# The second norm's gain: from the token rows to the experts' transposed tiles, and a second buffer for the normed rows

## The chip, the cores and the metric

The kernel runs on one core of a Trainium2 chip. The metric is the device time of one execution in microseconds (us); the median of three runs of the kernel before is 1646.28 us. The engines are named as in the profile: PE (TensorE), PEld (its weight loads), DVE (VectorE), ACT (ScalarE), POOL (GpSimd) and SP (the sync engine, which here issues most DMAs).

## What is computed

Two transformer blocks stand one after the other on 512 tokens of width 1024. The change touches the end of the second block, cut here to what matters:

```
x = x + u @ w_out                                  # output projection and residual
h = x * rsqrt(mean(x*x) + eps) * g                 # second norm, g = norm2_g (1024 weights)
logits = h @ w_router + b                          # 4 groups, 32 experts
y = sum over the token's two experts of weight * ((silu(h @ w_gate[e]) * (h @ w_up[e])) @ w_down[e])
x = x + y
```

Each token goes to two of 32 experts. An expert has 6 MB of f32 weights (gate, up and down), so that all of them are about 200 MB that stream once from HBM.

## The kernel before

**Output projection and norm (lines 1208 to 1377).** The projection runs in two column halves `c` (line 1375: `c = 0`, line 1376: `c = 1`) over four token tiles `t` of 128 tokens. For each tile `ev_o(c)` (lines 1281 to 1318) is called when the last matmul has been issued: DVE adds the PSUM result to the residual in `x2` (line 1285, called the evacuation below), ACT squares it and sums (1286), PE transposes it (`transpose4`, line 258, four matmuls), ACT copies the transpose out (1307), and PE multiplies it with the router's weights (1296, eight matmuls to a tile); for `c = 1` DVE adds the two halves' logits (1300) and scales them by the row's `rs` (1301). `rs` comes from DVE (line 251) and a power on POOL (line 252).

**Normed rows.** At `c = 1` the tile also gets a buffer `h`, with one copy in the pool (`bufs=1`). POOL multiplies its first 512 columns by the gain (line 1290) and DVE the other 512 (line 1291); `normed_rows` (lines 1273 to 1279) then scales it by `rs` in place on ACT, in two steps, writes it to the DRAM tensor `h_d` by a DMA on POOL's queue (1278), and writes the un-normed `x2` rows to the output by a DMA on ACT's queue (1279). The buffer of tile `t + 1` can be written only when the DMA of tile `t` has read it.

**Routing.** `route(a, b)` (lines 1328 to 1353) picks the experts of tiles `a` to `b - 1` on DVE, and `places` (1355 to 1372) gives every token its slot in its expert's list. Tiles 0 to 2 are routed when the logits of tile 2 are there (line 1303), tile 3 afterwards. The slot lists `gi` (line 1500) say which rows of `h_d` an expert reads.

**Experts (lines 1406 to 1655).** Weights come through SP's queue in units of 2 MB, two DMAs each (`fetch`, line 1402), into a ring of ten unit buffers (`RING = 10`). Six of the first ten lie where the projection's tiles lie or `x2` lies, so that their loads wait for those; from the eleventh unit on a load waits until PE has used the unit that lay in its buffer. For each expert POOL gathers its rows of `h_d` (line 1525, three in advance), PE transposes them (`expert_x`, 1544), DVE copies the transpose to `xT` (1547), PE multiplies with gate and up (1555) and with down (1580), and POOL adds the weighted result to the output by a scattering DMA (1532). Experts with more than 64 tokens do the same again for a second list (`gv`, `yv`). The first gathers wait for all four `h_d` writes and for `gi`. `overflow` (line 1663), for over 128 tokens in one expert, is built but not entered with these inputs.

The order on each engine is set by the program's scheduler from the dependences; PE's in the expert stage follows the code.

The lines around which all of this turns:

```
xg[t] = rt1.tile([P, D], F32, tag="h", bufs=1, name=f"h2_{t}")
nc.gpsimd.tensor_tensor(xg[t][:, 0:512], x2[:, t, 0:512], g_n2[:, 0:512], op=ALU.mult)
nc.vector.tensor_tensor(xg[t][:, 512:D], xc, g_n2[:, 512:D], op=ALU.mult)
```

Of the kernel before, what the change touches and what calls it, by code (L numbers as in the profile page):

```python
# [9 lines left out]
F32 = mybir.dt.float32  # L10
# [4 lines left out]
AF = mybir.ActivationFunctionType  # L15
ALU = mybir.AluOpType
# [4 lines left out]
P = 128  # L21
S = 512
NT = S // P
D = 1024
KD = D // P
# [62 lines left out]
def tile_kernel(tc, I, out, dbg=None, stop=None):  # L88
    nc = tc.nc
# [211 lines left out]
    def load_row(pool, ap, n, tag="grow", bufs=None):  # L301
        r = pool.tile([P, n], F32, tag=tag, bufs=bufs, name=f"row{uid()}")
        nc.sync.dma_start(r, row_bcast(ap, 0, n))
        return r
# [30 lines left out]
    for t in range(NT):  # L335
        for half in range(2):
            ps = transpose4(xt[t][:, half * 512:(half + 1) * 512])
            for j in range(4):
                k = half * 4 + j
                split(Ah[:, k, t * P:(t + 1) * P], Al[:, k, t * P:(t + 1) * P], ps[:, j * P:(j + 1) * P],  # L340
                      scale=gx[:, k:k + 1])
    for t in range(NT):
        h = hpool.tile([P, D], F32, tag="h", bufs=2, name=f"h{uid()}")
# [439 lines left out]
    for i, nm in enumerate(("attn_q_gain_2", "attn_k_gain_2")):  # L783
        for k in range(2):
# [25 lines left out]
                                     ap=[[512, 8], [-1, P], [1, 384]]))  # L810
# [120 lines left out]
    for dl in range(1, 4):  # L931
        n = NT - dl
        nc.vector.tensor_tensor(B[dl][:, :, 0:n, :], B[dl - 1][:, :, 0:n, :], tot[:, :, dl - 1:dl - 1 + n, :],
                                op=ALU.add)
# [236 lines left out]
    x2 = xp.tile([P, NT * D], F32, tag="unit", name="x2").rearrange("p (t d) -> p t d", t=NT)  # L1171
# [37 lines left out]
    SLOTS = 64  # L1209
# [22 lines left out]
    rb = rt1.tile([P, 36], F32, name="rb")  # L1232
    nc.sync.dma_start(rb[:, 0:4], row_bcast(I["b_router_group_2"], 0, 4))
    nc.sync.dma_start(rb[:, 4:36], row_bcast(I["b_router_expert_2"], 0, 32))
    g_n2 = load_row(rt1, I["norm2_g_2"], D, bufs=1)
    LG = rtp.tile([P, NT, 36], F32, name="LG")
    h_d = dram.tile([S, D], F32, name="h_d")

# [32 lines left out]
    s2 = rt1.tile([P, NT, 2], F32, name="s2")  # L1271

    def normed_rows(t):
        h = xg[t]
        for c_ in range(2):
            cl = slice(c_ * 512, (c_ + 1) * 512)
            nc.scalar.activation(h[:, cl], h[:, cl], AF.Copy, scale=rs[t])
        hw[0] = nc.gpsimd.dma_start(h_d[t * P:(t + 1) * P, :], h)
        nc.scalar.dma_start(out[0, t * P:(t + 1) * P, :], x2[:, t, :])

    def ev_o(c):

        def ev(t, ps):
            xc = x2[:, t, c * 512:(c + 1) * 512]
            nc.vector.tensor_tensor(xc, xc, ps, op=ALU.add)
            nc.scalar.activation(ps, xc, AF.Square, accum_out=s2[:, t, c:c + 1])
            hT = rt1.tile([P, 4, P], F32, tag="hT", bufs=2, name=f"hT2_{t}{c}")
            if c == 1:
                xg[t] = rt1.tile([P, D], F32, tag="h", bufs=1, name=f"h2_{t}")
                nc.gpsimd.tensor_tensor(xg[t][:, 0:512], x2[:, t, 0:512], g_n2[:, 0:512], op=ALU.mult)  # L1290
                nc.vector.tensor_tensor(xg[t][:, 512:D], xc, g_n2[:, 512:D], op=ALU.mult)

            def logits():
                lp_ = bank("s")
                for k in range(4):
                    nc.tensor.matmul(lp_[:, 0:36], hT[:, k, :], wr[:, c * 4 + k, :], start=k == 0, stop=k == 3)
                if c == 0:
                    nc.vector.tensor_copy(LG[:, t, :], lp_[:, 0:36])
                    return
                nc.vector.tensor_tensor(LG[:, t, :], LG[:, t, :], lp_[:, 0:36], op=ALU.add)  # L1300
                nc.vector.scalar_tensor_tensor(LG[:, t, :], LG[:, t, :], rs[t], rb, op0=ALU.mult, op1=ALU.add)
                if t == NT - 2:
                    route(0, NT - 1)

            def post():
                tp = transpose4(xc)
                copied = nc.scalar.activation(hT.rearrange("p j t -> p (j t)"), tp, AF.Copy)
                later(logits, 1)
                if c == 1:
                    with tc.issue_after(copied.ins):  # L1310
                        normed_rows(t)
            later(post, 1)
            if c == 0:
                return
            ss = small.tile([P, 1], F32, tag="ss", name=f"ss{uid()}")
            nc.vector.tensor_tensor(ss, s2[:, t, 0:1], s2[:, t, 1:2], op=ALU.add)
            rs[t] = rstd(ss, 1, 1.0 / D)
        return ev
# [52 lines left out]
        nc.vector.tensor_reduce(pj[:, qa:qb], prod, axis=AX.X, op=ALU.add)  # L1371
        onehots(0, io64, range(qa, qb))

    rs, hw, xg = {}, [None], {}
    run(lin_tok(A, wo_, [(0, 512)], ev_o(0), W=per_row(wo_u), beat=2))
    run(lin_tok(A, wo_, [(512, 512)], ev_o(1), W=per_row([wout(u, 1) for u in range(4)]),
                beat=2))
# [161 lines left out]
    def expert_x(xs, xT=None):  # L1539

        xv = xs.rearrange("s (p j) -> s j p", j=4)
        tp = tr_bank("xt")
        for j in range(4):
            nc.tensor.transpose(tp[:, j * P:(j + 1) * P], xv[:, j, :], ident)  # L1544
        if xT is None:
            xT = mp.tile([P, 4, P], F32, tag="xT", bufs=2, name=f"xT{uid()}")
        nc.vector.tensor_copy(xT.rearrange("p j s -> p (j s)"), tp)  # L1547
        return xT

    def gu_half(ps, xT, W, h):  # L1550
# [109 lines left out]
    tb_i = dram.tile([NE, P], I32, name="tb_i")  # L1660
    tb_w = dram.tile([NE, P], F32, name="tb_w")

    def overflow(blk):
        tb = ops.tile([P, 512], F32, tag="tr", name=f"tb{blk}")
        onehots(blk * P, iota, range(2 * NT))
# [6 lines left out]
        with tc.For_i(0, NE, 1) as i:  # L1672
# [9 lines left out]
            for half in range(2):  # L1682
                tp = ops.tile([P, 512], F32, tag="tr", name=f"otp{blk}{half}")
                for j in range(4):
                    nc.tensor.transpose(tp[:, j * P:(j + 1) * P], xv[:, half * 4 + j, :], ident)
                nc.vector.tensor_copy(xT[:, half * 4:half * 4 + 4, :].rearrange("p j s -> p (j s)"), tp)
            gu = []
            for nm, w_ in (("g", wg_d), ("u", wu_d)):
                w = op.tile([P, KD, 512], F32, tag="w" + nm, name=f"ow{nm}{blk}")
# [64 lines left out]
```

## Time and profile before

| what | value |
|---|---|
| runs | 1644.40, 1646.28, 1648.93 us; median 1646.28 |
| the profiled execution | 1646.24 us, its span 1644.5 us |
| PE busy | 1510.2 us (92%) |
| DVE, ACT, POOL busy | 695.5 us (42%), 537.3 us (33%), 200.7 us (12%) |
| DMA | 320.91 MB, mean 195 GB/s |
| DMA share in the last 12 of 40 slices | 90% or more but for the very last |

The span is what the hardware profiler recorded; the execution's own time is 1.7 us longer than it. Busy shares are averages over stages with different limits: the first two thirds are matmuls at full rate, the last third is the stream of expert weights. A releaser in brackets or behind an arrow is what ended an engine's idle time.

### The profile page before, as it was taken

What the parts mean: (1) busy time and instruction counts of PE and PEld (TensorE: products, weight loads), DVE (VectorE), ACT (ScalarE), POOL (GpSimd) and SP (SyncE); (2) the same over time, 40 slices, a digit from 0 to 9 for tenths busy, and PEclk for the clock granted to TensorE, in tenths of its full rate; (3) what the DMA queues carried; (4) which work ended last, traced back from release to release, by engine and by line L of the source; (5) the groups of instructions that cost most, each with busy time, mean ns of one, the idle gap of its engine ahead of it and who ended that gap; (6) DMA issues with size and microseconds to landing.
All of it is one profiled execution on the core that took longest, in us unless ns stands there. A gap on an engine that the chain in (4) does not pass through costs nothing. (4 is left out here: it accounts for less than half of the span.)

```text
span 1644.5 us, 20717 instructions
## 1 busy us (share of the span) xinstructions
PE 1510.2 (92%) x7446; PEld 1044.7 (64%) x7446; DVE 695.5 (42%) x1545; ACT 537.3 (33%) x1044; POOL 200.7 (12%) x196
## 2 busy tenths in 40 slices
PE   7999999889999999989999999993989999998875
PEld 7887776688888888778888778783333333333231
DVE  7699636663334454556884454624100100000000
ACT  6444437742234343344454543231111011111000
POOL 1000001220000000140000000003222222322211
PEclk9999999999999999999999999996999999999998
DMA  5313105013333332234222235397799999999995
GB/s 175 116 52 90 40 26 179 27 52 102 103 103 103 103 102 91 84 103 149 89 71 65 83 110 208 105 386 292 295 406 412 408 410 409 402 409 409 412 414 213
DMA packets 100064, 320.91 MB, mean 195 GB/s; under 512 B 18532, under 2 KB 27316, under 8 KB 75362
## 3 DMA queue, kind: packets, MB, share of 16 engines
q1 hardware_dynamic: 88626, 306.63, 50.0%
q0 software_dynamic: 10736, 10.54, 2.6%
q10 hardware_dynamic: 576, 2.10, 0.3%
q8 instruction: 75, 1.23, 0.3%
q14 instruction: 51, 0.42, 0.1%
HBM read 317.07 MB, written 21.25 MB: 206 GB/s over the span
## 5 line engine op out<-in xcount | busy, mean ns | idle before, releaser
L126 PE MATMUL mm<-wh,Ah 128*128 128x512 f32 (+3 forms) x800 | 307.8, 385 | 7.5 <-ACT wh L132 3.7
L127 PE MATMUL mm<-wl,Ah 128*128 128x512 f32 (+3 forms) x800 | 299.8, 375 | 1.2 <-DVE wl L133 1.2
L128 PE MATMUL mm<-wh,Al 128*128 128x512 f32 (+3 forms) x800 | 299.7, 376 | 0.0
L1555 PE MATMUL gu<-mr,xT 128*64 128x512 f32 x1024 | 240.4, 611 | 36.4 <-DMA mr<-in_w_expert_up_dram 21.4
L133 DVE TENSOR_TENSOR wl<-raw,wh 128x1024 fp32r<-128x1024 f32 (+3 forms) x160 | 184.8, 1162 | 118.2 <-ACT wh L132 114.8
L132 ACT ACTIVATE wh<-raw 128x1024 fp32r<-128x1024 f32 (+3 forms) x164 | 163.9, 1008 | 143.9 <-PE mm L127 108.6
L1555 PEld LDWEIGHTS gu<-mr,xT 128*64 128x64 f32 x1024 | 77.3, 140 | 174.4 <-issue 169.1
L126 PEld LDWEIGHTS mm<-wh,Ah 128*128 128x128 f32 x800 | 152.5, 191 | 34.3 <-ACT wh L132 4.8
L126 PE MATMUL mm<-Ah,wh 128*128 128x512 f32 x416 | 169.4, 407 | 0.0
L127 PEld LDWEIGHTS mm<-wl,Ah 128*128 128x128 f32 x800 | 153.0, 191 | 24.8 <-DVE wl L133 2.2
L128 PEld LDWEIGHTS mm<-wh,Al 128*128 128x128 f32 x800 | 152.3, 191 | 25.7 <-DVE Al L133 0.7
L128 PE MATMUL mm<-Ah,wl 128*128 128x512 f32 x416 | 163.2, 392 | 0.0
L127 PE MATMUL mm<-Al,wh 128*128 128x512 f32 x416 | 163.2, 392 | 0.0
L1547 DVE COPY xT<-xt 128x512 f32<-128x512 f32 x35 | 24.2, 692 | 307.1 <-PE xt L1544 307.1
L252 POOL TENSOR_TENSOR rr<-rm,mhalf 128x1 f32<-128x1 f32 (+3 forms) x40 | 32.5, 813 | 920.8 <-DVE rm L251 917.5
L1580 PE MATMUL yy<-mr,aT 128*64 128x512 f32 x512 | 116.9, 597 | 9.7 <-PEq L1643 8.4
L1580 PEld LDWEIGHTS yy<-mr,aT 128*64 128x64 f32 x512 | 39.4, 136 | 85.4 <-issue 81.2
L127 PEld LDWEIGHTS mm<-Al,wh 128*128 128x128 f32 x416 | 78.3, 188 | 17.6 <-issue 2.9
L126 PEld LDWEIGHTS mm<-Ah,wh 128*128 128x128 f32 x416 | 78.4, 188 | 17.2 <-issue 2.9
L1532 POOL DMA_INDIRECT out_dram<-ys,gi x35 | 56.3, 1608 | 268.0 <-ACTq L1606 202.7
L128 PEld LDWEIGHTS mm<-Ah,wl 128*128 128x128 f32 x416 | 78.3, 188 | 15.9
L1572 ACT ACTIVATE aT<-at 128x256 f32<-128x256 f32 x35 | 13.4, 382 | 160.5 <-PE at L1570 160.3
(370 smaller groups left out, 1860.4 us busy)
## 6 DMA issues: line engine op xcount, KB each, us to landing
mr<-in_w_expert_gate_dram SPq DMA_DIRECT2D x64, 1024.0 KB, 21.0
mr<-in_w_expert_up_dram SPq DMA_DIRECT2D x64, 1024.0 KB
mr<-in_w_expert_down_dram SPq DMA_DIRECT2D x64, 1024.0 KB, 21.2
raw<-in_w_in_dram SPq DMA_DIRECT2D x56, 512.0 KB, 3.6
raw<-in_w_up_dram SPq DMA_DIRECT2D x32, 512.0 KB, 3.7
raw<-in_w_down_dram SPq DMA_DIRECT2D x32, 512.0 KB, 4.1
raw<-in_w_out_dram SPq DMA_DIRECT2D x16, 512.0 KB, 4.3
gate_d<-gt SPq DMA_DIRECT2D x16, 256.0 KB, 2.9
```

Source lines behind the costliest of these rows:

```text
L126: nc.tensor.matmul(ps, ah, bh, start=first, stop=False)
L127: nc.tensor.matmul(ps, ah, bl, start=False, stop=False)
L128: nc.tensor.matmul(ps, al, bh, start=False, stop=last)
L132: nc.scalar.activation(hi, src, AF.Copy)
L133: return lo_eng.tensor_tensor(lo, src, hi.bitcast(F32), op=ALU.subtract)
L252: nc.gpsimd.tensor_tensor(r[:, :n], m[:, :n], mhalf[:, :n], op=ALU.pow)
L1532: nc.gpsimd.indirect_dma_start(out=dst, out_offset=bass.IndirectOffsetOnAxis(ap=idx, axis=0), in_=ys, in_offset=None, bounds_check=n - 1, ...
L1547: nc.vector.tensor_copy(xT.rearrange("p j s -> p (j s)"), tp)
L1555: last = nc.tensor.matmul(ps[c * 64:(c + 1) * 64, :].rearrange("s (w f) -> s w f", w=2), xT[:, j, h * 64:(h + 1) * 64], wv[:, :, j, c * 25 ...
L1572: nc.scalar.activation(aT.rearrange("p j s -> p (j s)"), tp[:, 0:256], AF.Copy)
L1580: nc.tensor.matmul(ps[c * 64:(c + 1) * 64, :], aT[:, j, h * 64:(h + 1) * 64], wv[:, h, j, c * 512:(c + 1) * 512], start=h + j == 0, stop=h ...
```

## The change

The gain is no longer multiplied into the normed rows. `normed_rows` makes the rows in one ACT step from `x2` into a buffer `h` with two copies, and the write of `x2` to the output is issued behind that step. The POOL and DVE multiplications and the load of the gain as a row on all partitions go. Instead the gain is applied where an expert's tokens have been transposed: the copy to `xT` becomes a multiplication by `g_x`, a tile of 4 by 2 gains to a partition that is repeated along the slots. `g_x` is loaded as single elements on SP's queue. The `overflow` code gets its own gain tile `g_o`, loaded at the end whether that code is entered or not. The router's weights had the gain multiplied in before and are not touched.

```
-    g_n2 = load_row(rt1, I["norm2_g_2"], D, bufs=1)
+    g_ap = I["norm2_g_2"]
+
+    def gain(pool, J, hs, nm):
+
+        g_ = pool.tile([P, J, hs], F32, name=nm)
+        nc.sync.dma_start(g_, bass.AP(tensor=g_ap.tensor, offset=g_ap.offset, ap=[[J, P], [1, J], [D // hs, hs]]))
+        return g_
+
+    g_x = gain(rtp, 4, 2, "g_x")
...
     def normed_rows(t):
-        h = xg[t]
-        for c_ in range(2):
-            cl = slice(c_ * 512, (c_ + 1) * 512)
-            nc.scalar.activation(h[:, cl], h[:, cl], AF.Copy, scale=rs[t])
+
+        h = rt1.tile([P, D], F32, tag="h", bufs=2, name=f"h2_{t}")
+        rows = nc.scalar.activation(h, x2[:, t, :], AF.Copy, scale=rs[t])
         hw[0] = nc.gpsimd.dma_start(h_d[t * P:(t + 1) * P, :], h)
-        nc.scalar.dma_start(out[0, t * P:(t + 1) * P, :], x2[:, t, :])
+        with tc.issue_after(rows.ins):
+            nc.scalar.dma_start(out[0, t * P:(t + 1) * P, :], x2[:, t, :])
...
-            if c == 1:
-                xg[t] = rt1.tile([P, D], F32, tag="h", bufs=1, name=f"h2_{t}")
-                nc.gpsimd.tensor_tensor(xg[t][:, 0:512], x2[:, t, 0:512], g_n2[:, 0:512], op=ALU.mult)
-                nc.vector.tensor_tensor(xg[t][:, 512:D], xc, g_n2[:, 512:D], op=ALU.mult)
...
-        nc.vector.tensor_copy(xT.rearrange("p j s -> p (j s)"), tp)
+        nc.vector.tensor_tensor(xT.rearrange("p j (h s) -> p j h s", h=2), tp.rearrange("p (j h s) -> p j h s", j=4, h=2),
+                                g_x[:, :, :, None].to_broadcast([P, 4, 2, SLOTS]), op=ALU.mult)
...
+    g_o = gain(op, KD, 1, "g_o")
...
-                nc.vector.tensor_copy(xT[:, half * 4:half * 4 + 4, :].rearrange("p j s -> p (j s)"), tp)
+                nc.vector.tensor_tensor(xT[:, half * 4:half * 4 + 4, :], tp.rearrange("p (j s) -> p j s", j=4),
+                                        g_o[:, half * 4:half * 4 + 4, :].to_broadcast([P, 4, P]), op=ALU.mult)
```

How the instructions stand, at three places. POOL, tiles 2 and 3 of the last projection half, before (`h_2` and `h_3` are the normed rows, `row` the gain, `rr` the power that gives `rs`, `xs` the first gather's buffer):

```order
L1290 TENSOR_TENSOR h_2_9496<-x_8767,row_9142 128x512
L252 TENSOR_TENSOR rr_9502<-rm_9501,mhalf 128x1
L1278 DMA h_d<-h_2_9496 128x1024
L1290 TENSOR_TENSOR h_3_9568<-x_8767,row_9142 128x512
L252 TENSOR_TENSOR rr_9574<-rm_9573,mhalf 128x1
L1278 DMA h_d<-h_3_9568 128x1024
L1590 MEMSET xs_9743 128x512
```

and POOL at the same place with the change:

```order
L252 TENSOR_TENSOR rr_9493<-rm_9492,mhalf 128x1
L1285 DMA h_d<-h_2_9509 128x1024
L252 TENSOR_TENSOR rr_9562<-rm_9561,mhalf 128x1
L1285 DMA h_d<-h_3_9571 128x1024
L1595 MEMSET xs_9731 128x512
```

The multiplication that stood ahead of each power is gone; nothing takes its place on POOL.

DVE, from the last step of routing tiles 0 to 2 over the evacuation of tile 3 (the row with `mm`) to that tile's logits, before (`ss` and `rm` lead to `rs`; `ohe`, `ohs`, `rec` and `recw` are routing work of tiles 0 to 2):

```order
L1347 TENSOR_TENSOR eid<-eid,gix 128x6
L1285 TENSOR_TENSOR x_8767<-x_8767,mm_9505 128x512
L1349 TENSOR_TENSOR ohe<-iota,eid 128x192
L1291 TENSOR_TENSOR h_3_9568<-x_8767,row_9142 128x512
L1353 TENSOR_TENSOR ohs<-ohe 128x96
L1316 TENSOR_TENSOR ss_9571<-s_9174 128x1
L1365 TENSOR_TENSOR rec<-ohe,tokc 128x192
L251 TENSOR_SCALAR rm_9573<-ss_9571 128x1
L1300 TENSOR_TENSOR LG<-LG,s_9587 128x36
L1369 TENSOR_TENSOR recw<-ohe,s_9175 128x64
L1301 SCALAR_TENSOR_TENSOR LG<-LG,rr_9574,rb 128x36
```

and DVE at the same place with the change:

```order
L1351 TENSOR_TENSOR eid<-eid,gix 128x6
L1293 TENSOR_TENSOR x_8767<-x_8767,mm_9496 128x512
L1353 TENSOR_TENSOR ohe<-iota,eid 128x192
L1357 TENSOR_TENSOR ohs<-ohe 128x96
L1369 TENSOR_TENSOR rec<-ohe,tokc 128x192
L1320 TENSOR_TENSOR ss_9559<-s_9174 128x1
L251 TENSOR_SCALAR rm_9561<-ss_9559 128x1
L1304 TENSOR_TENSOR LG<-LG,s_9575 128x36
L1373 TENSOR_TENSOR recw<-ohe,s_9175 128x64
L1305 SCALAR_TENSOR_TENSOR LG<-LG,rr_9562,rb 128x36
```

The write into `h_3` is gone from between the evacuation and the statistics; the evacuation still stands behind the routing of tiles 0 to 2.

SP, where the small constants and the first loads of the output projection's weights (`raw`) are issued, as a piece of the difference:

```order
 L148 DMA raw_9014<-in_w_branch_mlstm_dram 128x2x512
-L1243 DMA iota<-in_cst_dram 128x128
-L1245 DMA io_9148<-in_cst_dram 128x128
-L1247 DMA half_9150<-in_cst_dram 128x1
-L1249 DMA tokc<-in_cst_dram 128x4
-L1255 DMA recw<-in_cst_dram 128x128
+L1240 DMA g_x<-in_norm_g_dram 128x8x1
+L1251 DMA iota<-in_cst_dram 128x128
+L1253 DMA io_9148<-in_cst_dram 128x128
+L1255 DMA half_9150<-in_cst_dram 128x1
+L1257 DMA tokc<-in_cst_dram 128x4
+L1263 DMA recw<-in_cst_dram 128x128
```

The load of `g_x`, 8 single elements to each of 128 partitions, stands ahead of five small loads and of the `w_out` loads behind them; the row load of the gain, further down in the same queue, is gone.

## Rows read from the trace of the kernel before

**Rows 1.** Stretches: length, busy us of engines, PEclk, DMA share, GB/s.

```profile
1036.50:1039.00 2.50, 2.50 (x13) 2.00 (x12) 1.80 (x4) 0.63 (x1) 0.00 (x0) 1.00 1.06 227
1108.00:1113.00 5.00, 4.33 (x20) 3.25 (x19) 2.86 (x6) 0.74 (x2) 1.86 (x2) 1.00 0.02 10
1119.00:1149.00 30.00, 7.24 (x42) 6.35 (x42) 15.40 (x82) 4.29 (x9) 9.26 (x13) 0.58 0.95 353
1149.50:1161.00 11.50, 8.19 (x28) 3.15 (x30) 2.04 (x4) 0.42 (x1) 3.76 (x4) 0.63 0.21 50
1180.00:1460.00 280.00, 257.09 (x1179) 95.88 (x1180) 24.21 (x44) 30.64 (x65) 74.52 (x60) 1.00 1.02 408
1460.00:1600.00 140.00, 115.13 (x508) 42.77 (x506) 10.01 (x18) 13.77 (x28) 32.55 (x26) 0.97 1.02 412
```

**Rows 2.** Timeline of SP's queue, weight loads: start, us, instruction.

```profile
1118.66 0.33 SPq L1414 DMA_DIRECT2D mr<-in_w_expert_gate_dram  x1
...
1159.63 0.81 SPq L1414 DMA_DIRECT2D mr<-in_w_expert_down_dram  x2
```

**Rows 3.** SP's waits, 1060 to 1170: us in total, times, longest.

```profile
SPq L148 <- DVE wl L133: 30.6, 4, 25.6
SPq L1414 <- DMA out_dram<-x: 22.1, 3, 11.1
SPq L1414 <- PEq L1624: 16.1, 1, 16.1
```

**Rows 4.** Timeline of POOL: start, us, instruction, idle before it.

```profile
1101.56 0.79 POOL L1278 DMA_DIRECT2D h_d<-h  x1 [1.69 <-ACT h L1277]
...
1121.47 0.61 POOL L1278 DMA_DIRECT2D h_d<-h  x1 [1.66 <-ACT h L1277]
...
1134.93 0.60 POOL L1278 DMA_DIRECT2D h_d<-h  x1 [1.66 <-ACT h L1277]
...
1145.23 1.12 POOL L1525 DMA_INDIRECT xs<-h_d,gi  x1 [7.16 <-DVE wgt L1468]
```

**Rows 5.** Timeline of PE, tile 2's transposes and the first expert's matmuls.

```profile
1113.17 0.66 PE L258 MATMUL t<-ident,x 128*128 128x128 f32 x4 [0.84 <-DVE x L1285]
...
1153.75 5.75 PE L1555 MATMUL gu<-mr,xT 128*64 128x512 f32 x16 [0.78 <-DVE xT L1547]
```

**Rows 6.** Timeline of DVE, tiles 0 to 3 of the projection's second half.

```profile
1097.35 0.69 DVE L1285 TENSOR_TENSOR x<-x,mm 128x512 f32<-128x512 f32 x1 [2.64 <-PE mm L128]
...
1101.64 0.26 DVE L1301 SCALAR_TENSOR_TENSOR LG<-LG,rr,rb 128x36 f32<-128x36 f32 x1
1104.18 0.69 DVE L1285 TENSOR_TENSOR x<-x,mm 128x512 f32<-128x512 f32 x1 [2.29 <-PE mm L128]
...
1119.84 0.26 DVE L1301 SCALAR_TENSOR_TENSOR LG<-LG,rr,rb 128x36 f32<-128x36 f32 x1 [0.64 <-POOL rr L252]
...
1122.82 0.68 DVE L1285 TENSOR_TENSOR x<-x,mm 128x512 f32<-128x512 f32 x1
...
1130.23 1.76 DVE L1291 TENSOR_TENSOR h<-x,row 128x512 f32<-128x512 f32 x1 [6.47 <-DMA h_d<-h]
...
1133.30 0.26 DVE L1301 SCALAR_TENSOR_TENSOR LG<-LG,rr,rb 128x36 f32<-128x36 f32 x1 [0.51 <-POOL rr L252]
...
1140.39 0.25 DVE L1500 TENSOR_SCALAR gi<-t,half 128x32 int32<-128x32 f32 x1 [0.71 <-PE t L1476]
```

**Rows 7.** Groups of DVE by line and shape: busy us, mean ns, idle before.

```profile
L1547 DVE COPY xT<-xt 128x512 f32<-128x512 f32 x35 | 24.2, 692 | 307.1 <-PE xt L1544 307.1
...
L395 DVE TENSOR_TENSOR t<-mm,cs 128x512 f32<-128x512 f32 x16 | 11.0, 687 | 22.4 <-PE mm L128 22.4
...
L1291 DVE TENSOR_TENSOR h<-x,row 128x512 f32<-128x512 f32 x4 | 6.0, 1512 | 15.0 <-DMA h_d<-h 15.0
```

**Rows 8.** The DMAs that write or read h_d, time to landing.

```profile
DMA to landing us min/median/max: 2.2/7.0/9.4
```

**Rows 9.** SP's waits, 1600 to the end.

```profile
SPq L1750 <- DMA out_dram<-ys,gi: 9.2, 1, 9.2
```

More of the change, by code (lines that the diff above doesn't have):

```diff
@@ L1372, in places @@
         onehots(0, io64, range(qa, qb))
-    rs, hw, xg = {}, [None], {}
+    rs, hw = {}, [None]
     run(lin_tok(A, wo_, [(0, 512)], ev_o(0), W=per_row(wo_u), beat=2))
```

## The prediction, made before the changed kernel ran

> **What bounds the kernel now.** I read the page's slices first, where DMA share is full for the last third, then cut that third into stretches [rows 1]. From 1180 to 1460 us, and again to 1600, the DMA share stays at 1.02 and 408 to 412 GB/s: the stage moves expert weights as fast as DMA goes anywhere in this trace, while PE has some slack (257.1 of 280 us busy, then 115.1 of 140). The end of the kernel is therefore the moment from which this stream runs without holes, plus a fixed amount of bytes. So the place to look is where the stream has holes ahead of 1180. There are two. One is 1108 to 1113 (share 0.02): the next unit buffer is still read by the output projection, and its load starts only at 1118.66 [rows 2]. The other is 1149.5 to 1161 (share 0.21): all ten unit buffers are full, SP waits 16.1 us for PE [rows 3], and the next load goes out at 1159.63 [rows 2], when PE has done the first 16 matmuls of the first expert. Those began at 1153.75 and took 5.75 us [rows 5]: PE had little to do before (7.2 of 30 us), and its granted clock there is 0.58 and 0.63, mostly the lower of its two levels, 1.2 GHz [rows 1].
>
> So what is late is PE's first expert. It needs the first gather, which POOL issues at 1145.23 [rows 4]. The gather needs the slot list, there at 1140.64, and the last write of normed rows, issued at 1134.93: it waits for the write. Both are late for one reason. Of tiles 0 to 3 on DVE [rows 6], the second evacuation follows the first by 6.83 us, PE's pace; but tile 3's comes at 1122.82, not at 1117.84, and its logits end in a step at 1133.30, 10.48 us behind, where tile 0 needed 4.29. In between DVE sits 6.47 us until the DMA of the previous tile's rows has read the only buffer; over the tiles this costs DVE 15.0 us of waiting [rows 7].
>
> **The change, part by part.**
>
> *Multiplications into the buffer.* Four on POOL and four on DVE go, and with them the wait for the buffer. DVE had run late since tile 1, and PE stood 0.84 us for it [rows 5]; that goes too. New times, from tile 0's undisturbed steps [rows 4, 6]. Evacuation of tile 2: 1104.18 + 6.83 = 1111.01. Its logits' last step: + 4.29 = 1115.30. Routing of tiles 0 to 2 stays ahead of tile 3 on DVE and takes 1122.82 - 1119.84 = 2.98, so tile 3's evacuation comes at 1118.28, behind its PSUM at 1117.84. Its logits: 1122.57, which is 10.7 us earlier. The slot list: 1140.64 - 1133.30 = 7.34 later, 1129.91. The write of its rows: tile 0 took 1101.56 - 1097.35 = 4.21, so 1122.49, which is 12.4 us earlier.
>
> *One ACT step in place of two, from x2.* It does the same 1024 columns, inside the 4.21 just used; I count nothing, and at most it saves a part of that. Its result goes into one of two buffers: tile 3 wants the one that tile 1's write (issued about 1108.4) reads, 12 us after that; the slowest write seen took 10.3 (below).
>
> *Landing of the last write.* Not shown for the new conditions. Issued at 1121.47, tile 2's let DVE go at 1130.23, 8.8 us; tile 3's let the gather go 10.3 us after 1134.93 [rows 4, 6]. I take 8.8: like the new one it starts when the weight loads have just resumed. The gather goes at 1131.25, 14.0 us earlier; with 10.3 at 1132.79, 12.4 earlier; if the write were quick the slot list would decide, 1129.91, 15.3 earlier.
> The Trainium skill, SBUF — State Buffer, section "SBUF: two separate sides", says that a DMA from GpSimd's queue has its descriptors written by GpSimd, and that VectorE work on the shared ports keeps it from writing them. VectorE runs the same dense routing work beside the new write as beside the old one, so by this rule the landing stays at 10.3 and the time comes out at about 1635.0. The 8.8 of tile 2, which had VectorE idle for most of it, does not contradict that.
>
> *The gather's own flight.* From issue to the first expert's matmuls 1153.75 - 1145.23 = 8.5 us. Now it falls wholly among weight loads, where before these ended soon after. DMAs on h_d land in 7.0 us (median), at most 9.4 [rows 8]; I add 1.2, bounds 0 and 2.8. PE's first expert starts 12.8 us earlier, near 1141, still at the lower clock since PE again has some 20 us with little to do, and the first buffer is free at 1146.8.
>
> *What the stream can take of it.* Starting PE earlier pays only while the ring is full. The hole is worth 11.5 x (1 - 0.21) = 9.1 us. The fill ends earlier, too: PE's last matmul by 0.84, and tile 2's two writes of 0.5 MB (rows and output) now go out about 1115, in the empty stretch, rather than from 1119 on, up to 1.05 MB / 353 GB/s = 3.0 us; but SP still waits for output writes ahead of some weight loads (22.1 us [rows 3]), and tile 3's comes only some 2 us earlier, behind the ACT step. So the stream can use 11.1 to 12.9 us. Path and stream meet at nearly one value; I take 12.2.
>
> *xT as a multiplication.* DVE's copy from PSUM takes 692 ns, a two-operand step from PSUM with a repeated operand 687 [rows 7]: nothing. The repeat is along the innermost axis here, which that row does not have; bound 1.8 us, a step of this size beside POOL (1.76 [rows 6]), so 1.1 once on the path of the first expert. Later ones are covered by PE's work and by the stream. *Loads.* `g_x` is 1024 single elements; two loads that together have 2048 pieces took 2.5 us [rows 1]. It stands ahead of the `w_out` loads, but later in that queue SP waits 25.6 us for DVE anyway [rows 3]. Without that cover it would cost its 2.5. The row load of 512 KB that goes lies ahead of the first hole, and saves nothing. `g_o`, 4 KB, is issued behind the last weight load and lands while the last scatter is under way, for which SP waits 9.2 us [rows 9].
>
> *Sum.* Against the profiled execution's own time: 1646.24 - 12.2 = 1634.0 us. The median of the runs shown is 1646.28, the same.
>
> **The rivals.**
> 1. *Slower: the first rows stand behind the weights.* The writes of the output rows land earlier, so SP is let go earlier and puts more weight loads ahead of the last write and the first gathers. If these were served behind them, landing plus gather would exceed the 10.3 + 8.5 us they had, and from 10.3 + 8.5 + 12.4 = 31.2 us on PE would start later than now. At twice the old figures, 37.6, that is 6.4 us more: 1652.6. Against it: no DMA on h_d, in a stage with the DMA full, took over 9.4 [rows 8]. The Trainium skill, DMA: Bandwidth & Descriptors, section "Queues, rings and completion order", has each DMA engine take turns between queues, which also speaks against it.
> 2. *No change: the same, but only up to 27 to 31 us.* The wait moves from the buffer to the DMA and eats the gain: 1642 to 1646, middle 1644. The write's 10.3 us, three times the time that 0.5 MB needs at 353 GB/s plus some, show that writes do wait among the weights.
> 3. *The change does less than it says:* only tile 3's own wait goes (6.47 + 1.76 us), while its evacuation stays late because routing stands ahead of it on DVE: 8.2 less the 1.2 of the gather, 7.0, 1639.2. Against it: routing was late through tile 2's wait, which goes too.
>
> **How the numbers follow.** A measurement of this kernel can tell about 0.3%, 5 us, from no change. Forecast 0.74: its ends are a gain of 9.6 (10.3 to land, 2.8 in flight) and of 15.3 (the slot list decides), 1631 to 1636.6; runs lie 2.3 us about the median, so 1629 to 1639. Rival 3 has 0.10, rival 2 0.10, rival 1 0.05, and 0.01 is left. Taking in rival 3 with its spread gives 1629 to 1641. Faster: forecast, rival 3 and a little of rival 2, 0.85; the same 0.10; slower 0.05.
>
> **What would show it.** After the change DVE should have no wait for a DMA of h_d; tile 3's evacuation near 1118, its row write near 1122, the first gather at 1131 to 1133, the first expert near 1141, and the next load after the ring is full near 1147, with the hole at 1150 nearly gone and the stages after it shifted as a block. The forecast is wrong if the first gather stays within 5 us of 1145, if its flight is over 15 us, or if the shift shrinks between 1180 and the end, which would mean that something other than the stream bounds that stage.

## The result, and the profile after

The changed kernel takes 1635.74 us in the median (1633.74 to 1638.64, five runs), the kernel before 1646.78 us over five runs: a ratio of 0.9933 with a 95% interval from 0.9916 to 0.9951. That is 11 us faster; 1634.0 was forecast, in a range from 1629 to 1641. The profiled execution took 1633.74 us, its span 1632.0 us.

The stretches of [rows 1] in the changed kernel, in the same columns:

```profile
1108.00:1113.00 5.00, 5.00 (x26) 4.12 (x25) 1.14 (x4) 1.33 (x4) 0.83 (x2) 1.00 0.34 138
1119.00:1149.00 30.00, 14.97 (x73) 8.91 (x74) 13.15 (x60) 2.60 (x7) 11.65 (x15) 0.60 0.90 346
1149.50:1161.00 11.50, 10.63 (x50) 5.35 (x48) 3.01 (x12) 2.34 (x5) 1.37 (x2) 0.85 0.86 322
1180.00:1460.00 280.00, 256.44 (x1176) 95.29 (x1173) 23.78 (x43) 31.24 (x66) 74.56 (x60) 1.00 1.02 408
...
1129.00:1132.00 3.00, 2.37 (x12) 2.26 (x11) 2.18 (x12) 0.00 (x0) 0.00 (x0) 0.50 0.19 77
```

The hole of 1149.5 to 1161 is filled (DMA share 0.86, it was 0.21), and the long stage behind it is the same as before (1.02, 408 GB/s): it only starts earlier. A small hole is new, at 1129 to 1132 (0.19).

DVE in the changed kernel: the evacuations of tiles 0, 2 and 3, tile 3's logits and the slot list; in its queue no wait for a DMA of `h_d` is left:

```profile
1096.75 0.69 DVE L1293 TENSOR_TENSOR x<-x,mm 128x512 f32<-128x512 f32 x1 [2.64 <-PE mm L128]
...
1110.41 0.69 DVE L1293 TENSOR_TENSOR x<-x,mm 128x512 f32<-128x512 f32 x1 [2.27 <-PE mm L128]
...
1117.69 0.68 DVE L1293 TENSOR_TENSOR x<-x,mm 128x512 f32<-128x512 f32 x1
...
1121.69 0.25 DVE L1305 SCALAR_TENSOR_TENSOR LG<-LG,rr,rb 128x36 f32<-128x36 f32 x1
...
1129.98 0.25 DVE L1504 TENSOR_SCALAR gi<-t,half 128x32 int32<-128x32 f32 x1 [0.71 <-PE t L1480]
```

The same stretch on POOL (the writes of the rows of tiles 2 and 3, the first gather), on PE (the first expert) and on SP (weight loads):

```profile
1114.44 0.58 POOL L1285 DMA_DIRECT2D h_d<-h  x1 [1.48 <-ACT h L1284]
...
1121.70 0.58 POOL L1285 DMA_DIRECT2D h_d<-h  x1 [1.48 <-ACT h L1284]
...
1132.08 1.10 POOL L1529 DMA_INDIRECT xs<-h_d,gi  x1 [7.40 <-DVE ohp L1328]
```

```profile
1140.86 5.29 PE L1560 MATMUL gu<-mr,xT 128*64 128x512 f32 x16 [0.78 <-DVE xT L1551]
```

```profile
1117.01 0.33 SPq L1418 DMA_DIRECT2D mr<-in_w_expert_gate_dram  x1
...
1131.42 0.43 SPq L1418 DMA_DIRECT2D mr<-in_w_expert_gate_dram  x1
...
1146.29 0.81 SPq L1418 DMA_DIRECT2D mr<-in_w_expert_down_dram  x2
```

Up to the output projection all kernels do the same work but for a few loads, yet tile 0's evacuation falls anywhere from 1096.75 to 1100.29 in the profiles. So I count from it. Then the first gather comes at 35.3 us (1132.08 - 1096.75; 47.9 before), the next load behind the full ring at 49.5 (62.3 before) and the span's end at 535.3 (547.2 before): 12.5, 12.7 and 11.9 us earlier. What PE's first expert gained, the stream took almost whole. The profile puts the first gather's wait down to DVE's `ohp` steps for the next list. But the same kernel, run again, issues the gather before the last of these is done (1132.36 and 1132.53), so I read the write of tile 3's rows as its release: issued at 1121.70, it landed 9.5 us later.

Two more views of the changed kernel answer to [rows 7]: DVE's multiplication into `xT` by its line, and who waited for a DMA on `h_d` between 1090 and 1150. Only PE is left, for the gathered tokens; before, DVE waited 15.0 us.

```profile
L1551 DVE TENSOR_TENSOR xT<-xt,g_x x35: 690/692/692, 1140.1 to 1591.1; 128x512 f32<-128x512 f32 x35
```

```profile
who waited for it (us, times):
  PE xt L1548: 6.5, 1
```

### The profile page after: what moved, and what is told of

It reads as the page before. It is cut to its first block, busy times and chain, and to the rows that moved or that the text cites. A ratio compares the mean times of both kernels' runs of the same rounds, so it can differ in the third digit from the quotient of the medians.

```text
span 1632.0 us, 20703 instructions
## 1 busy us (share of the span) xinstructions
PE 1511.7 (93%) x7446; PEld 1045.6 (64%) x7446; DVE 691.1 (42%) x1541; ACT 537.0 (33%) x1040; POOL 195.5 (12%) x192
## 5 line engine op out<-in xcount | busy, mean ns | idle before, releaser
L1560 PE MATMUL gu<-mr,xT 128*64 128x512 f32 x1024 | 241.9, 615 | 35.6 <-DMA mr<-in_w_expert_up_dram 19.8
L1551 DVE TENSOR_TENSOR xT<-xt,g_x 128x512 f32<-128x512 f32 x35 | 24.2, 691 | 304.0 <-PE xt L1548 304.0
```

What stands on the lines that cost most here:

```text
L1551: nc.vector.tensor_tensor(xT.rearrange("p j (h s) -> p j h s", h=2), tp.rearrange("p (j h s) -> p j h s", j=4, h=2), g_x[:, :, :, None].to ...
L1560: last = nc.tensor.matmul(ps[c * 64:(c + 1) * 64, :].rearrange("s (w f) -> s w f", w=2), xT[:, j, h * 64:(h + 1) * 64], wv[:, :, j, c * 25 ...
```

## The experiments

| kernel | median us | ratio to before, 95% | first gather | next load | end of span |
|---|---|---|---|---|---|
| before | 1646.78 | | 47.9 | 62.3 | 547.2 |
| the change | 1635.74 | 0.9933 [0.9916, 0.9951] | 35.3 | 49.5 | 535.3 |
| the change, again | 1635.54 | 0.9935 [0.9923, 0.9947] | 35.0 | 49.7 | 535.1 |
| 1 two copies, gain kept | 1639.40 | 0.9954 [0.9940, 0.9967] | 37.5 | 52.6 | 537.6 |
| 2 change, one copy | 1637.21 | 0.9932 [0.9919, 0.9946] | 34.9 | 49.9 | 535.1 |
| 3 change, one copy, row load kept | 1635.44 | 0.9920 [0.9906, 0.9933] | 35.6 | 50.8 | 535.4 |
| 4 gain behind the scaling | 1643.70 | 0.9976 [0.9966, 0.9987] | 36.9 | 52.5 | 541.3 |
| 5 the same, SP's order mended | 1644.90 | 0.9984 [0.9973, 0.9994] | 47.4 | 59.3 | 544.9 |
| 6 slot list later | 1643.32 | 0.9979 [0.9969, 0.9988] | 43.2 | 57.1 | 542.2 |
| 7 queues swapped | 1636.24 | 0.9940 [0.9926, 0.9953] | 35.4 | 49.7 | 536.0 |
| 8 both writes on POOL | 1635.24 | 0.9918 [0.9905, 0.9932] | 34.9 | 49.6 | 534.3 |
| 9 matmuls while waiting | 1633.72 | 0.9909 [0.9894, 0.9923] | 35.0 | 47.7 | 533.5 |
| 10 8 and 9 | 1634.85 | 0.9914 [0.9900, 0.9927] | 34.8 | 47.7 | 532.9 |
| 11 10 and earlier slots | 1633.11 | 0.9923 [0.9910, 0.9937] | 34.5 | 46.7 | 532.7 |

The last three columns are us behind tile 0's evacuation, each from the kernel's one profile. Every ratio is to the runs of the kernel before on the same chip, where their median lies between 1646.78 and 1648.18 us; so rows are compared by their ratios.

### Which part of the change made it: runs 1 to 5

Run 1, two copies, with both multiplications still there:

```
-    g_n2 = load_row(rt1, I["norm2_g_2"], D, bufs=1)
+    g_n2 = load_row(rt1, I["norm2_g_2"][0:512] if len(I["norm2_g_2"].shape) == 1 else I["norm2_g_2"][:, 0:512], 512, bufs=1)
...
-                xg[t] = rt1.tile([P, D], F32, tag="h", bufs=1, name=f"h2_{t}")
+                xg[t] = rt1.tile([P, D], F32, tag="h", bufs=2, name=f"h2_{t}")
...
-                nc.vector.tensor_tensor(xg[t][:, 512:D], xc, g_n2[:, 512:D], op=ALU.mult)
+                nc.vector.tensor_tensor(xg[t][:, 512:D], xc, g_n2[:, 0:512], op=ALU.mult)
```

> The kernel before with one thing changed: the buffer of normed rows has two copies. Both multiplications by the gain stay; so that the second copy fits, the gain's row holds its first 512 values only, which serve both column halves (the output is off by that). Theory A, the lateness came from DVE's wait for the single buffer: that wait (15.0 us before) is gone, tile 3's evacuation comes near 1118 instead of 1122.8, its row write near 1123 to 1124, the first gather near 1133 to 1134, and the time is 1636 to 1638, most of the change's gain. Rival B, the multiplications themselves are what cost: they stay, so the time stays within 3 us of 1646. Rival C, half and half: 1640 to 1642.

It got 7.6 us of the 11 (0.0046 of 1647.5); counted from tile 0's evacuation, in its one profile, 9.6 of 11.9. DVE's wait is gone, but part of it came back on POOL, whose order now has the next tile's multiplication ahead of the power that the tile at hand needs:

```profile
1110.79 1.29 POOL L1290 TENSOR_TENSOR h<-x,row 128x512 f32<-128x512 f32 x1 [7.12 <-DMA h_d<-h]
1112.05 0.57 POOL L252 TENSOR_TENSOR rr<-rm,mhalf 128x1 f32<-128x1 f32 x1
1114.31 0.61 POOL L1278 DMA_DIRECT2D h_d<-h  x1 [1.69 <-ACT h L1277]
1117.41 1.28 POOL L1290 TENSOR_TENSOR h<-x,row 128x512 f32<-128x512 f32 x1 [2.49 <-DMA h_d<-h]
```

So tile 3's evacuation comes 23.6 us behind tile 0's (1122.23 - 1098.64), between 25.5 before and 20.9 with the change. The wait for the single buffer was most of the cost, as theory A had it, but the time is a little worse than its range.

Run 2, the change with one copy:

```
-        h = rt1.tile([P, D], F32, tag="h", bufs=2, name=f"h2_{t}")
+        h = rt1.tile([P, D], F32, tag="h", bufs=1, name=f"h2_{t}")
```

> The changed kernel with one copy of the buffer of normed rows instead of two. Theory A: the buffer is now written by one ACT step late in each tile and no longer by DVE and POOL in the middle of it, and the write of tile 2's rows lands some 3 us after its issue at 1114.4, so tile 3 does not find the buffer taken; ACT may wait 1 or 2 us for it at tiles 1 and 2, the first gather moves by less than 1.5 us from 1132.1, and the time is 1635 to 1637.5. Rival B, the second copy is what made the change: the time goes back towards the kernel before, 1642 to 1646, with ACT waiting several us for a DMA of h_d.

Theory A holds (the gather at 34.9, the time in its range). But the free memory moved other loads in the projection's first half, and tile 0's evacuation came 3.5 us later than in the changed kernel's profile. That the loads did this is not shown: run 5 has it as late (1100.12) with the projection of the kernel before. So run 3 gives the second copy's memory back to the gain's row:

```
+    load_row(rt1, I["norm2_g_2"], D, bufs=1)
```

> The changed kernel with one copy of the buffer, and with the gain's row load of 512 KB kept (into a tile of the second copy's size that nothing reads). In the run with one copy alone the freed memory moved loads in the first half of the projection; here the order of all engines' work is the changed kernel's, but for that load. Theory A, neither the second copy nor the load's bytes matter, because what counts is who writes the buffer and when: first gather 35 to 36 us behind tile 0's evacuation (35.3 in the changed kernel, 47.9 in the kernel before), time 1635 to 1637. Rival B, the second copy does matter and the run with one copy hid it by its other order: gather 2 us later or more, time 1638 or above.

ACT, the scaling of the rows of tiles 0 to 3 in run 3:

```profile
1101.65 1.15 ACT L1285 ACTIVATE h<-x,rr 128x1024 f32<-128x1024 f32 x1
1112.03 1.15 ACT L1285 ACTIVATE h<-x,rr 128x1024 f32<-128x1024 f32 x1 [3.65 <-DMA h_d<-h]
1116.62 1.15 ACT L1285 ACTIVATE h<-x,rr 128x1024 f32<-128x1024 f32 x1 [1.47 <-DMA h_d<-h]
1122.61 1.15 ACT L1285 ACTIVATE h<-x,rr 128x1024 f32<-128x1024 f32 x1 [0.54 <-POOL rr L252]
```

Tiles 1 and 2 wait for the one buffer, 3.65 and 1.47 us; tile 3, the one that counts, does not. It takes 1635.44 us, and its span ends 535.4 us behind tile 0's evacuation against 535.3, which is theory A: once the multiplications are gone, neither the second copy nor the row's 512 KB is worth anything that can be measured. The single ACT step and the new place of the output write have no run of their own.

From this I expected that only the place of the write into the buffer matters, and turned the order round in the kernel before: ACT scales first, late in the tile, then POOL multiplies in place (run 4).

```
-        h = xg[t]
-        for c_ in range(2):
-            cl = slice(c_ * 512, (c_ + 1) * 512)
-            nc.scalar.activation(h[:, cl], h[:, cl], AF.Copy, scale=rs[t])
+        h = rt1.tile([P, D], F32, tag="h", bufs=1, name=f"h2_{t}")
+        nc.scalar.activation(h, x2[:, t, :], AF.Copy, scale=rs[t])
+        nc.gpsimd.tensor_tensor(h, h, g_n2, op=ALU.mult)
...
-            if c == 1:
-                xg[t] = rt1.tile([P, D], F32, tag="h", bufs=1, name=f"h2_{t}")
-                nc.gpsimd.tensor_tensor(xg[t][:, 0:512], x2[:, t, 0:512], g_n2[:, 0:512], op=ALU.mult)
-                nc.vector.tensor_tensor(xg[t][:, 512:D], xc, g_n2[:, 512:D], op=ALU.mult)
```

> The kernel before (gain still in the normed rows, one buffer), with the order inside a tile turned round: ACT first writes the buffer from the un-normed rows, scaled, in one step late in the tile, and POOL then multiplies all 1024 columns by the gain in place; DVE has no part in it. Theory A, what made the kernel before late is that DVE and POOL took the buffer in the middle of the tile, ahead of what else they had to do: with ACT taking it late, DVE does not wait, tile 3's evacuation comes 21 us behind tile 0's as in the changed kernel (25.5 before), the row write goes 2.5 us later than there for POOL's multiplication, the first gather 37 to 39 us behind tile 0's evacuation (35.3 changed, 47.9 before), and the time is 1637.5 to 1640. Rival B, the gain had to leave the rows, or a second copy was needed: gather above 43 us, time 1643 to 1647.

The gather came early, as theory A had it (36.9), but the time did not follow (1643.70). The program's scheduler had put SP's read of the token counts ahead of loads that fill the ring. SP's wait there, and the stretch 1118 to 1134 (columns as in [rows 1]):

```profile
SPq L1613 <- DVE ohp L1319: 36.8, 1, 36.8
```

```profile
1118.00:1134.00 16.00, 5.19 (x35) 4.47 (x34) 12.23 (x49) 2.47 (x4) 8.96 (x10) 0.63 0.30 121
```

The stream stood for most of 16 us. Run 1's load behind the ring goes at nearly the same time (52.6, here 52.5), and it ends 3.7 us sooner (537.6, here 541.3). An early first expert is of little use when the weights are not there. Run 5 holds that read back, on top of run 4's edit:

```
+    ring_last = wload[0].ins
...
+    lead = ExitStack()
+    lead.enter_context(tc.issue_after(ring_last))
     for i in range(NE + 1):
+        if i == 1:
+            lead.close()
```

> The run with POOL's multiplication behind ACT's scaling once more, with SP's load of the experts' token counts held behind the loads of the first ten units; in that run it stood ahead of three of them, so that SP waited 36.8 us for DVE and the stream stood still from 1118 to 1134. Theory A, that gap alone took the gain away: now the stream runs again while the last row write lands, so this write takes 9 to 10 us instead of 7, the first gather goes 39 to 41 us behind tile 0's evacuation (47.9 before, 35 with the change), the first 16 matmuls are done at 54 to 56 us (62.3 before, 49.6 with the change), and the time is 1638.5 to 1641.5, in proportion. Rival B, the gain in the rows costs the whole of it in some other way: 1643 to 1647 with the gather where theory A has it.

The loads run again, and now the wait for the buffer is back, on ACT (tiles 2 and 3):

```profile
1119.60 1.15 ACT L1275 ACTIVATE h<-x,rr 128x1024 f32<-128x1024 f32 x1 [3.37 <-DMA h_d<-h]
...
1134.31 1.15 ACT L1275 ACTIVATE h<-x,rr 128x1024 f32<-128x1024 f32 x1 [8.65 <-DMA h_d<-h]
```

Both theories fall short: the gather is at 47.4, not 40, and here the profile names its release, the last write of the rows:

```profile
1147.51 1.12 POOL L1522 DMA_INDIRECT xs<-h_d,gi  x1 [6.27 <-DMA h_d<-h]
```

The time is in rival B's range, but with the late gather of the kernel before, and not with theory A's. The rows of tile 2 go out 23.4 us behind tile 0's evacuation (1123.47 - 1100.12), after the weight loads have started again, and that write takes 10.8 us to land. With the change the same write is issued at 17.7 (1114.44 - 1096.75), while the loads still wait for the projection (they start at 20.3, 1117.01), and lands in 3.0:

```profile
h_d<-h POOLq DMA_DIRECT2D x1, 512.0 KB, 3.0
```

```profile
h_d<-h POOLq DMA_DIRECT2D x1, 512.0 KB, 10.8
```

(the first is the changed kernel's issue at 1114.44, the second run 5's at 1123.47). So one buffer is enough when tile 2's write is out before the loads resume. In neither of the two orders tried here was it, with the multiplications on the way to it; other orders with the gain in the rows were not tried. With the gain where it was, a second copy gives two thirds.

### What the end hangs on: run 6

The first slot list is computed 32 times over:

```
-            routed = nc.vector.tensor_scalar(g_, rows, -2.0, half2[:, 0:1], op0=ALU.mult, op1=ALU.add)
+            for _ in range(1 if blk else 32):
+                routed = nc.vector.tensor_scalar(g_, rows, -2.0, half2[:, 0:1], op0=ALU.mult, op1=ALU.add)
```

> The changed kernel in which DVE computes the first slot list 32 times over instead of once (same values). The slot list is ready about 6 us later, near 1136, and with it the first gather, near 1136.5 instead of 1132.1, 4.4 us later. Theory A, the ring of buffers is full and the stream waits for PE's first expert, so the path from the gather sets the end: first expert 4.4 us later, time 1639 to 1641. Rival B, the path has slack, and the stream itself (its holes at 1130 to 1132 and before 1117) sets the end: the time stays within 1.5 us of 1635.7.

The 32 steps and the gather behind them:

```profile
1130.66 9.11 DVE L1505 TENSOR_SCALAR gi<-t,half 128x32 int32<-128x32 f32 x32 [0.72 <-PE t L1480]
```

```profile
1140.63 1.19 POOL L1530 DMA_INDIRECT xs<-h_d,gi  x1 [15.26 <-DVE ohp L1328]
```

The delay was larger than meant, 7.9 us at the gather (43.2 - 35.3), and so the time lies above theory A's range. It is 7.6 at the next load and 6.9 at the end of the span; the medians differ by 7.6. The hole is open again (1146 to 1156, columns as in [rows 1]):

```profile
1146.00:1156.00 10.00, 7.72 (x28) 3.06 (x30) 2.67 (x8) 0.42 (x1) 2.99 (x3) 0.68 0.20 56
```

Theory A's mechanism holds: with the ring full, the first gather sets the end nearly one to one.

### What is left on that path: runs 7 to 11

Run 7, each tile's two writes on each other's queue:

```
-        hw[0] = nc.gpsimd.dma_start(h_d[t * P:(t + 1) * P, :], h)
+        nc.scalar.dma_start(h_d[t * P:(t + 1) * P, :], h)
...
-            nc.scalar.dma_start(out[0, t * P:(t + 1) * P, :], x2[:, t, :])
+            hw[0] = nc.gpsimd.dma_start(out[0, t * P:(t + 1) * P, :], x2[:, t, :])
```

> The changed kernel with the two DMAs of each tile on each other's queue: the normed rows are written from ACT's queue, the output rows from POOL's. Theory A, the last row write, 9.5 us from issue to landing, releases the first gather, and it is slow because it goes through POOL's queue (its first packets move 3.9 us after the issue, those of ACT's queue about 2 us after): it lands 1 to 2 us earlier, the first gather goes at 1130.4 to 1131, where the slot list decides, and the time falls by 0.5 to 1.5 us to 1634 to 1635. Rival B, it is slow because weight loads are ahead of it on the DMA engines, whatever the queue: landing 8.5 to 9.5, gather within 0.7 us of 1132.1, time 1635 to 1636.5.

ACT's issue of the last rows, and the first gather:

```profile
1122.91 0.33 ACTq L1285 DMA_DIRECT2D h_d<-h  x1
```

```profile
1133.63 1.13 POOL L1529 DMA_INDIRECT xs<-h_d,gi  x1 [9.60 <-DVE den L1470]
```

10.7 us from one to the other, as from POOL's queue (1132.08 - 1121.70 = 10.4): rival B, the queue is not what makes this write slow. The 2 us that the expectation gives ACT's queue from issue to first packets do not hold here: by stretches of 0.2 us in the changed kernel's trace, tile 3's output write waits 3.7 us (1120.26 to 1124.0) on ACT's queue, its row write 4.3 (1121.70 to 1126.0) on POOL's. Run 7 also shows that the slot list does not set this gather. With POOL's MEMSETs earlier it is there 31.6 us behind tile 0's evacuation (1098.20), where the change has 33.5, and the gather stays at 35.4:

```profile
1129.53 0.25 DVE L1504 TENSOR_SCALAR gi<-t,half 128x32 int32<-128x32 f32 x1 [0.72 <-PE t L1480]
```

Run 8 leaves the rows on POOL's queue and puts the output write behind them there:

```
-        with tc.issue_after(rows.ins):
-            nc.scalar.dma_start(out[0, t * P:(t + 1) * P, :], x2[:, t, :])
+        with tc.issue_after(hw[0].ins):
+            hw[0] = nc.gpsimd.dma_start(out[0, t * P:(t + 1) * P, :], x2[:, t, :])
```

> The changed kernel with the output rows' writes moved from ACT's queue to POOL's, each issued behind the normed rows' write. Theory A, the last row write is slow to land because the output rows' write, issued 1.4 us ahead of it, and the weight loads share the DMA engines with it: it lands 1 to 2.5 us sooner, the first gather goes when the slot list is there, 1 to 1.8 us sooner (33.5 to 34.3 us behind tile 0's evacuation), and SP no longer waits for an output write ahead of the second down load, so the gap at 1130 to 1132 closes: time 1633 to 1635. Rival B, the gathers now stand behind the last output rows' write in the same queue: gather sooner, but its flight 1.5 us longer or more, time 1635.5 to 1638.

Its two stretches that matter:

```profile
1129.00:1132.00 3.00, 0.95 (x9) 0.94 (x9) 2.42 (x15) 0.00 (x0) 0.00 (x0) 0.50 1.02 426
1146.00:1150.00 4.00, 3.84 (x16) 1.37 (x14) 0.23 (x1) 0.00 (x0) 0.78 (x1) 0.81 0.11 24
```

The gap at 1129 to 1132 is closed: it was SP waiting for an output write. The bytes came earlier, the ring was full earlier, and the gap is now at 1146 to 1150. The gather gained 0.5 us (0.1 against the change run again), where theory A had 1 to 1.8, and its flight is not longer (8.8), which speaks against rival B. It now follows the slot list by 0.85 us, as in run 6 (0.86), so here the slot list sets it, and that came 0.5 us later than in the change. The first 16 matmuls took 5.87 us (5.29 in the change), so the next load goes no sooner (49.6), and the median gained nothing that can be told.

Run 9 adds 34 small matmuls on PE, 16 ahead of tile 3's slots and 18 ahead of the first expert:

```
+    def warm(ps, n):
+        for _ in range(n):
+            nc.tensor.matmul(ps[:, 0:P], ident, ident, start=True, stop=True)
...
+    warm(bank("t"), 16)
...
+    warm(tr_bank("warm"), 18)
```

> The changed kernel with 34 small matmuls (identity by identity into a bank that nothing reads) on PE while it waits for routing and for the first gather. Theory A, the first expert runs at the lower clock because PE had little to do before, and the stream waits for its first 16 matmuls: these take 3.7 to 4.3 us in place of 5.29, the next load goes 1 to 1.6 us sooner, time 1633.5 to 1635. Rival B, the stream has no more to gain there (the gap that was left between 1146 and 1160 is not this one's): the matmuls are faster but the time stays 1635 to 1637. Rival C, the clock does not rise by so little work: 5.2 us, time unchanged.

The first expert, and the stretch around it (columns as in [rows 1]):

```profile
1142.53 3.65 PE L1565 MATMUL gu<-mr,xT 128*64 128x512 f32 x16 [0.78 <-DVE xT L1556]
```

```profile
1139.00:1147.00 8.00, 6.91 (x41) 4.15 (x40) 0.69 (x1) 0.00 (x0) 2.44 (x3) 0.95 1.02 409
```

The 16 matmuls take 3.65 us in place of 5.29; the granted clock of this stretch is 0.95, mostly 2.4 GHz, where the changed kernel has 0.68. In the other profiles of kernels with the change and without these matmuls the 16 take 5.21 to 6.14 us. The next load goes 1.9 us earlier and the span ends 1.8 earlier: theory A. In runs 9 to 11 that load goes at 46.7 to 47.7, in the profiles of the change and of runs 2, 3, 7 and 8 at 49.5 to 50.8. The median is in theory A's range, but the interval of the ratio overlaps with the change's (0.9894 to 0.9923 and 0.9916 to 0.9951). Run 10 has both edits; run 11 has `places(0, NT - 1)` right behind `route(0, NT - 1)` as well.

> The changed kernel with both: the output rows' writes behind the normed rows' on POOL's queue, and the 34 small matmuls on PE. Theory A, both act on the one path that the stream waits for, so their gains add up until the gaps between 1129 and 1160, 4.4 us in all, are closed: first 16 matmuls of the first expert done 2.5 to 3.5 us sooner (46 to 47 us behind tile 0's evacuation instead of 49.5), time 1631.5 to 1633.5. Rival B, the stream takes neither: 1635 to 1637.

> The kernel with the output rows' writes on POOL's queue and the 34 small matmuls, and with the slots of tiles 0 to 2 worked out as soon as these are routed, so that DVE and PE do a part of it in the 2 us in which they wait for tile 3's logits. Theory A, with the row write landing sooner the slot list sets the first gather: it is ready 1 to 1.5 us sooner, the gather goes 33.5 to 34.2 us behind tile 0's evacuation (34.8 without), the first 16 matmuls are done near 47 us, time 1632.5 to 1634.5. Rival B, the row write's landing still sets the gather, or the full ring of buffers takes the gain away: gather at 34.8, time as without, 1634 to 1635.5.

> The changed kernel once more, beside the two others on one chip, as the measure for differences of one or two us: 1634 to 1637.5, first gather 35 to 35.7 us behind tile 0's evacuation, first 16 matmuls of the first expert done at 49 to 50 us.

Run 10 missed both of its theories: the 16 matmuls are done 47.6 us behind tile 0's evacuation, as in run 9 (47.5), and 1634.85 us is above theory A's range and just under rival B's, so the two edits did not add up. In run 11 the slot list is there 2.5 us sooner than in run 10 (31.2 and 33.7), and the gather only 0.3 (34.5 and 34.8). So the landing of the rows sets it, as rival B had it, though the time is in theory A's range; the rest of what the next load gained on run 10 (46.7 and 47.7) came in the gather's flight (8.5 and 9.2). The changed kernel once more came as expected.

Counted from tile 0's evacuation run 11 ends 2.4 to 2.5 us ahead of the two profiles of the change, and its next load goes 2.8 to 2.9 earlier. Its median is 1633.11 against 1635.54 on the same chip; the intervals overlap (0.9910 to 0.9937 and 0.9923 to 0.9947), so by time alone it is not shown to be faster than the change. Both are faster than the kernel before.

## Why the prediction was right, point by point

*What bounds the kernel.* As forecast: the stages behind 1180 move as a block, run 6 shows that the first expert sets it, and run 4 that the full ring is the other half of the condition.

*Multiplications and buffer.* Tile 2's evacuation was forecast 13.66 us behind tile 0's and came at 13.66, tile 3's at 20.93 and 20.94, its row write at 25.14 and 24.95. The reason holds, with one correction: the text let the second copy carry tile 3, and run 3 shows that it isn't needed, since tile 2's write lands in 3.0 us.

*Slot list.* Forecast at 32.56 (1129.91 - 1097.35), measured 33.48. The logits' last step came 0.3 us early (24.94 where 25.22 was forecast), and the chain from there took 8.54 us in place of 7.34. One group in it is 1.5 us longer: the six steps that write `ohp` for tiles 0 to 2. Before:

```profile
1134.24 1.48 DVE L1324 TENSOR_SCALAR ohp<-io,pj 128x128 fp32r<-128x128 f32 x6
```

and with the change, where POOL clears the gather buffers at the same time (before, it began with that at 1135.53, when five of the six were done):

```profile
1122.62 2.99 DVE L1328 TENSOR_SCALAR ohp<-io,pj 128x128 fp32r<-128x128 f32 x6
```

```profile
1122.27 1.48 POOL L1595 MEMSET xs<- 128x512 f32 x3
1123.67 1.01 POOL L1595 MEMSET xb<- 128x512 f32 x2
```

From the slot list to the gather the sum counted nothing; where the list sets the gather, it is 0.85 us (runs 6 and 8).

*Landing and flight.* This is where I chose: 8.8 us for the landing; it was 10.4 to the gather's start. The chosen flight of 9.7 us was 8.8 (1140.86 - 1132.08). The two errors, 1.6 and 0.9, went against each other, and the first expert came at 44.1 where 43.6 was forecast: the landing was too short, the 1.2 added to the flight were not needed, and that the two nearly cancelled is luck. The sentence on the Trainium skill, SBUF — State Buffer, section "SBUF: two separate sides", had the better number, but run 7 speaks against its reason, which holds for GpSimd's queue only: from ACT's queue the write took 10.7 us. The nearest row for a write among weight loads was tile 3's own, and I should have taken it.

*The stream.* 12.2 us were forecast, 11.9 measured by the span from tile 0's evacuation. The lower end of the forecast's 11.1 to 12.9 is not worked out in it (the hole and PE's 0.84 alone make 9.9), and 12.2 is a choice between the ends. The hole is closed as forecast (0.21 to 0.86). Part of the 3.0 us at most that I gave tile 2's earlier writes was lost again, by my reading, in the new gap at 1129 to 1132 (2.4 us): SP waited for output writes 24.4 us in all, where 22.1 stood before.

```profile
SPq L1418 <- DMA out_dram<-x: 24.4, 2, 12.7
```

In run 8 the gap is closed and the next load goes no sooner (49.6), so it cost nothing that can be told from the time.

*Multiplication on `xT` and loads.* 692 ns in the median, as the copy took [rows 7]; the bound of 1.1 us is out. `g_x` takes SP 1.27 us to issue, and the load of the router's weights, some way behind it, goes out at 1035.16, where it went at 1035.40 before.

*Against the median.* The sum started from 1646.24 us; the forecast missed the median by 1.7 us, less than the runs lie apart (1633.74 to 1638.64). The profiled run's 1633.74 is the fastest of the five.

*The rivals.* Nothing landed late enough for rivals 1 and 2: landing and flight were 10.4 and 8.8 us, together 0.3 more than before, far from the 27 us where the second began. Rival 3 fell with tile 3's evacuation, which comes 4.5 us earlier behind tile 0's (20.9, it was 25.5).

## What to carry to other kernels

Where a stage streams weights through a ring, look at the moment when the ring is full and the consumer has not started: what delays the consumer's first step is then worth nearly its full length (run 6), and what fills the ring sooner still is worth nothing that could be told here (run 8), but a ring that isn't full by then costs too (run 4). A buffer's cost is in the transfer that empties it: the same 512 KB took 3.0 us in a pause of the stream and 10.8 in the stream, so moving a step off the way to that transfer did more here than a second copy (11 us and 7.6).

## What I had not expected of the hardware

The six `ohp` steps on DVE took 1.48 us alone and 2.99 beside POOL's MEMSETs (3.94 in run 8, 1.26 in run 11, where they come just ahead of the MEMSETs):

```profile
1122.10 1.26 DVE L1329 TENSOR_SCALAR ohp<-io,pj 128x128 fp32r<-128x128 f32 x6
```

All fourteen profiles fit: 1.26 to 1.48 us where the steps and the MEMSETs share at most 0.2 us (before, runs 5, 7 and 11), 1.71 with 0.75 us shared (run 4), 2.62 to 3.94 in the other nine. It is not the MEMSETs alone: eight more such steps take 1.65 to 1.68 us in the other profiles and 4.08 in run 5, where POOL multiplies tile 3's rows beside them:

```profile
1134.81 4.08 DVE L1319 TENSOR_SCALAR ohp<-io,pj 128x128 fp32r<-128x128 f32 x8
```

The Trainium skill, SBUF — State Buffer, section "SBUF: two separate sides", has a pair of ports that a VectorE step in a two-port mode and a GpSimd step lock against each other for a whole instruction; these rows agree with that, though no run here shows in which mode the DVE steps ran. No run moves the clearing of the buffers for its own sake, to an idle time of DVE.

And 34 matmuls that compute nothing, in a stretch where PE waited (15.05 us busy of the 20 from 1119, where the change alone has 5.92), brought the first expert to 2.4 GHz and the next load 1.9 us forward.
